# Weight casts queued beside other ScalarE work, and a weight load cut into quarters, in a streaming encoder layer

## The chip, the cores and the metric

The kernel runs on one core of a Trainium2 chip. The metric is the device time of one execution in microseconds (us); lower is better. The engines are named as in the profile: PE (TensorE, matrix multiplication; PEld is its weight load), ACT (ScalarE), DVE (VectorE), POOL (GpSimd) and SP (SyncE, which here only issues DMA transfers). Each engine works through its own queue in order.

## The reference

One layer of a streaming encoder, for 1024 prompt tokens and 8 decode streams of 16 tokens. The width is 1024; there are 8 heads of 64 with stick-breaking attention (group A) and 8 heads of 64 with banded chunk attention (group B).

```python
def trunk_layer(x, p, ...):
    h = rmsnorm(x, g_mix)
    q_a, k_a, v_a, q_b, k_b, v_b = split_heads(h, w_in)
    a = stick_breaking(q_a, k_a, v_a, ...)       # with the cached past for the decode streams
    o_b = band_attention(q_b, k_b, v_b, ...)
    a = rmsnorm(a, g_out_sb)
    o_b = rmsnorm(o_b, g_out_cb)
    x = x + concat(a, o_b) @ w_out
    h = rmsnorm(x, g_ffn)
    x = x + (silu(h @ w_gate) * (h @ w_up)) @ w_down
    gate = sigmoid(rmsnorm(x, g_ple) @ w_ple_gate)
    x = x + gate * (p @ w_ple_proj)
    return x, new

def stick_breaking(q, k, v, q_pos, k_pos):
    z = einsum('bqhd,bkhd->bhqk', q, k) * HEAD_DIM ** -0.5
    causal = k_pos[None, :] < q_pos[:, None]
    log_keep = where(causal, log_sigmoid(-z), 0.0)
    between = cumsum(log_keep, axis=3, reverse=True) - log_keep
    w = where(causal, exp(log_sigmoid(z) + between), 0.0)
    return einsum('bhqk,bkhd->bqhd', w, v)
```

## The kernel before

All data is float32. A product of two float32 matrices is made of three fast products: each operand is split into a high part, rounded by a cast (on ACT), and a low part, the difference (on POOL or DVE); `mm3` (L101 to L104) multiplies high by high, high by low and low by high. So every weight chunk costs a load into `wraw`, a cast to `whi` and a subtraction to `wlo`. A chunk is 128 x 2048 elements (1 MB); it is cast and subtracted in parts, mostly quarters of 128 x 512. There is one raw buffer, so the next load starts when the last subtraction has read the one before; there are two buffers of high and low parts.

The tokens are nine tiles of 128 rows: eight of the prompt, one that holds the decode streams. The stages, with their rough times in the profile:

- 0 to 130: norm of the rows, transposes, first chunks of the projection.
- 130 to 290: the other projection chunks (12 of 256 columns in all) beside the stick-breaking attention of the decode streams, `decode(0, ...)`. The order of PE is that of the code here; the other engines' orders come from a list scheduler with a model of times.
- 290 to 510: the last projection chunks beside the stick-breaking attention of the prompt, `attention` (`advance(project, att, 1.95)`). The scheduler orders all engines.
- 510 to 806: the banded attention of the decode streams and of the prompt and, beside the latter, the first half of the output product (`half_out`).
- 806 to 870: second half of the output product (`lower`), row by row, with the norm and the transposes for the next stage. PE's order is that of the code from the third row on.
- 870 to 1340: gate and up product; 1340 to 1590: down product; then the gate by the layer's input embedding and the final norm.

What the change touches:

- `Chunks.beside` (L162 to L176) runs a projection chunk's units (one unit is one product of a token tile, or of three for queries) and, from the second unit on, casts one quarter of the next chunk after each of four units (L174), with the subtraction on POOL. When the products of a unit are copied out of PSUM, ACT does it for every other tile (`st`, L296) and for the transposed keys and queries (`transposed_out`, L253 and L256).
- In the decode attention DVE weighs the scores (`wdec`, L463); POOL copies the last 16 columns to `wn` (L475), which PE transposes (L433).
- In the attention of the prompt POOL multiplies `w` by `keep` (L605, stick-breaking), or ACT takes the exponential (L607, banded), and PE transposes `w` (L623).
- `half_out` (L1002 to L1025) follows the string `ORDER`. "t" is a transpose of one head pair's mixed heads for three tiles (`turn_mix`: PE L867, then `hUh` on ACT L870 and `hUl` on DVE L871), "u0" and "u1" make a tile of the left or right 512 columns, a number such as "50" waits for head pair 5 and transposes its first group; "r" loads the second output weights (right columns), "p" casts and subtracts them in four parts.
- `lower` (L1092 to L1098) adds the second half of the output product to a tile `xa` or `xb` and stores it to `x1d`. Two rows later `weighed` multiplies `xa` by the norm's weights in place on POOL (L1109), so it must wait for that store. ACT takes the squares (`T4h`, L1104) and scales `hrow` (L1122), which PE transposes (L1130).
- `gate_up(0)` (L1220, load at L143) fetches the first gate chunk; `part_of` (L1081) casts it, one half at the eighth row and one at the end.

Of the kernel before, what the change touches and what calls it, by code (L numbers as in the profile page):

```python
# [13 lines left out]
F32 = mybir.dt.float32  # L14
# [8 lines left out]
P = 128  # L23
D = 1024
KT = 8
# [7 lines left out]
SKEW = 2  # L33
R2 = 1.2
LAG, RAWS, PT = 5, 7, 2
FIRST = 2
ORDER = ("u0 40 t u0 41 t u0 42 t t r u0 t u0 t t u0 t u0 p 50 u0 51 u0 52 "
         "u1 60 u1 61 u1 62 u1 u1 u1 u1 u1 u1")
VLAG, AHEAD = (2, 1), 2

# [2 lines left out]
def tile_hymba_step(  # L43
# [82 lines left out]
    def load_row(pool, src, tag):  # L126
        t_ = pool.tile([P, D], F32, name="row_" + tag, tag=tag)
        nc.sync.dma_start(t_, src.broadcast_to([P, D]))
        return t_

    class Chunks:


# [31 lines left out]
        def beside(self, units, src, k, n, first):  # L165

            v = self.raw(src, k, n)
            h, l = self.pair(k, n)
            for i, _ in enumerate(units):
                yield  # L170
                j = i - first
                if 0 <= j < 4:
                    o = slice(j * k // 4, (j + 1) * k // 4)
                    A.copy(h[:, o], v[:, o])  # L174
                    sub(G, l[:, o], v[:, o], h[:, o])
            return h, l  # L176

# [68 lines left out]
    def qkv(ch, hT, stg, first, second):  # L246

        def transposed_out(grp, w, c, g, src, scale=1.0):
            both = stg.tile([P, 2, 384], F32R, name="sq", tag="sq")
            n = min(384, NP * P - g * 384)  # L250
            hl = [both[:, x, :n] for x in range(2)]
            if scale == 1.0:
                A.copy(hl[0], src[:, :n])  # L253
                sub(V, hl[1], src[:, :n], hl[0])
            else:
                A.activation(hl[0], src[:, :n], AF.Copy, scale=scale)  # L256
                V.scalar_tensor_tensor(hl[1], src[:, :n], scale, hl[0].bitcast(F32), op0=ALU.mult, op1=ALU.subtract)
            for x in range(2):
                sent.append(nc.sync.dma_start(qkT[grp][w][x][c, :, g * 384 : g * 384 + n], hl[x].bitcast(F32)))
            if n < 384:  # L260
                new = both[:, 0, n:].bitcast(F32)
                A.activation(new, src[:, n:], AF.Copy, scale=scale)
                nc.sync.dma_start(fresh[grp][w][c], new)
# [23 lines left out]
        def others(grp, w, c, wts, gs):  # L287

            wh, wl = wts
            for g in gs:  # L290
                st = stg.tile([P, 3, 256], F32, name="st", tag="st", bufs=2)
                for o in range(3):
                    ps_ = ps["o"].tile([P, 256], F32, name="ps", tag="O")
                    for k in range(KT):
                        mm3(ps_, *hT.tok(g * 3 + o, k), wh[:, k], wl[:, k], k == 0, k == KT - 1)
                    (V.tensor_copy if o % 2 else A.copy)(st[:, o], ps_)  # L296
                    if w == 2 and g * 3 + o < NP:
                        values_out(grp, c, g * 3 + o, st[:, o])
                    yield
                if w == 1:  # L300
                    for pr in range(2):
                        pt = ps["t"].tile([P, 384], F32, name="pt", tag="T")
                        for o in range(3):
                            T.transpose(pt[:, o * P : (o + 1) * P], st[:, o, pr * P : (pr + 1) * P], ident)
                        transposed_out(grp, 1, c * 2 + pr, g, pt)
                first = 4 if grp else 0
                ts_ = [t for t in range(g * 3, g * 3 + 3) if first <= t < NP]
                if ts_:
                    lo, hi = ts_[0], ts_[-1] + 1
                    nc.sync.dma_start(  # L310
                        kv_prompt[grp, w][0, 0, (lo - first) * P : (hi - first) * P, c * 4 : c * 4 + 4, :]
                        .rearrange("(t p) h d -> p t (h d)", p=P),
                        st[:, lo - g * 3 : hi - g * 3],
                    )
                if g == 2:
                    nc.sync.dma_start(
                        kv_sample[grp, w][0, :, :, c * 4 : c * 4 + 4, :].rearrange("b i h d -> (b i) (h d)"),
                        st[:, 2],
                    )
                    if w == 2:  # L320
                        nc.sync.dma_start(fresh_v[grp][c], st[:, 2])
# [207 lines left out]
            yield  # L529


    kept, last = [], [None, None]

    def attention(ap_, ps, lag):
# [40 lines left out]
        def scores(st, hh, t):  # L575
# [28 lines left out]
                G.memset(w[:, n - 1 :], 0.0)  # L604
                kept.append(G.tensor_tensor(w[:, : n - 1], w[:, : n - 1], keep[:, 1:], op=ALU.mult))  # L605
            else:
                A.activation(w, w, AF.Exp, bias=mx, scale=-1.0, accum_out=st["rs"][:, hh, t : t + 1])  # L607
            return w

        def flip(st, hh, t, w):  # L610
# [390 lines left out]

    def half_out():  # L1002

        turns = [(k, g) for g in (1, 2) for k in range(4)]
        nc.sync.dma_start(own, mixs[1])
        late = [fetch_mix(k, 2) for k in range(3)]
        place = {0: 0, 1: 0}
        for what in ORDER.split():
# [5 lines left out]
                half_weights.append(out_raw(0, 1))  # L1014
                continue
            elif what == "p":
                half_weights[1] = ch.parts(half_weights[1], 4, 512, 4)
                continue
            elif what[0] == "u":
                c = int(what[1])  # L1020
# [66 lines left out]
    def fetch(t, half):  # L1087
        x = xg.tile([P, 512], F32, name="x" + "ab"[half], tag="x" + "ab"[half], bufs=(4, 2)[half])
        nc.sync.dma_start(x, resid[t * P : (t + 1) * P, half * 512 : half * 512 + 512])
        xs[t, half] = x  # L1090

    def lower(t, half):  # L1092
        acc = bank()
        for k in range(4):
            mm3(acc, *hT.tok(t, 4 + k), w_b[half][0][:, k], w_b[half][1][:, k], k == 0, k == 3)
        x = xs[t, half]
        V.tensor_tensor(x, x, acc, op=ALU.add)
        nc.sync.dma_start(x1d[t * P : (t + 1) * P, half * 512 : half * 512 + 512], x)  # L1098

    def squares_of(t, i, x):  # L1100
        if not i:
# [107 lines left out]
    with ExitStack() as planned:  # L1209
        for i in range(NT + SKEW):  # L1210
# [6 lines left out]
                fetch(order[j + 1], 1)  # L1217
            if i < NT:
                lower(order[i], 0)
            if i == SKEW:  # L1220
                raw = gate_up(0)
            if j < 0:
                continue
            if j == 1:
# [614 lines left out]
```

## Time and profile before

| what | value |
|---|---|
| median of 3 runs | 1699.58 us (1699.13 to 1699.96) |
| the profiled run | 1700.87 us |
| span of the profiled run | 1698.6 us |
| granted PE clock, mean over the span | 0.990 |
| instructions | 27811 |
| DMA, bytes moved | 292.44 MB |

The profile is of one execution. A row of a timeline gives start, duration, engine, line, operation, what is written and read, the shape and, in brackets, how long the engine stood idle before it and what ended the wait. A window's row gives its length, each engine's busy time with its count of instructions, the granted clock of PE as a share of full speed, the DMA engines' busy share and the rate. The idle time of an engine matters only where PE, which is nearly always busy, waits for it.

### The profile page before, as it was taken

How to read it: one execution, taken by the hardware profiler on the slowest of the kernel's cores; microseconds unless marked ns; L12 is line 12 of the kernel's file. 1: busy time of each engine (PE TensorE's matmuls, PEld its weight loads, DVE VectorE, ACT ScalarE, POOL GpSimd, SP SyncE). 2: the span in 40 equal slices, each digit the busy share in tenths (PEclk: the TensorE clock that was granted, in tenths of full speed). 3: DMA queues.
4: the chain of work that ended last, by engine and by line, in shares of the span. 5: the costliest groups of instructions: out<-in, count | busy, mean ns of one | idle time of the engine just before them, and what ended most of it. 6: DMA issues, size and time to landing. Idle time of an engine off the chain costs nothing.

```text
span 1698.6 us, 27811 instructions
## 1 busy us (share of the span) xinstructions
PE 1650.3 (97%) x10308; PEld 1420.7 (84%) x10308; DVE 1067.9 (63%) x1674; ACT 815.5 (48%) x1758; POOL 830.6 (49%) x691
## 2 busy tenths in 40 slices
PE   8999999989998999999999999999999999999998
PEld 7999788889997777888778888888888788788887
DVE  5111444258788766674676666566665597898875
ACT  5324445267767776573763333323333344433673
POOL 2433311178555321032675555555555379868763
PEclk9999999999998999999999999999999999999999
DMA  5877798665458896863522222222222697713222
GB/s 194 276 243 219 251 292 284 185 199 159 131 153 258 236 278 183 233 180 131 199 75 96 97 96 96 96 96 96 96 97 82 226 365 246 263 68 122 90 99 100
DMA packets 173145, 292.44 MB, mean 172 GB/s; under 512 B 16849, under 2 KB 95825, under 8 KB 170706
## 3 DMA queue, kind: packets, MB, share of 16 engines
q1 hardware_dynamic: 173010, 290.67, 52.8%
q8 instruction: 82, 1.34, 0.3%
q14 instruction: 53, 0.43, 0.1%
HBM read 204.24 MB, written 86.38 MB: 171 GB/s over the span
## 4 chain that ended last, share of the span: by engine, by line
PE 83%; DMA 5%; DVE 4%; ACT 3%; POOL 2%; issue 2%; SPq 0%; POOLq 0%; ACTq 0%; DVEq 0%
PE ps L1171 26%; PE ps L102 7%; PE ps L103 7%; PE ps L104 7%; PE pt L1444 4%; PE pt L1171 4%; PE ps L1444 3%; PE pt L623 3%; PE pt L424 2%; PE acc L487 2%; PE po L647 2%; PE po L646 2%; PE sdec L446 2%; PE S L592 1%; PE S L593 1%
## 5 line engine op out<-in xcount | busy, mean ns | idle before, releaser
L107 POOL TENSOR_TENSOR wlo<-wraw,whi 128x512 fp32r<-128x512 f32 (+1 forms) x143 | 225.5, 1602 | 66.2 <-ACT whi L161 34.7
L102 PE MATMUL ps<-whi,hTh 128*128 128x256 f32 x576 | 168.5, 293 | 0.0
L104 PE MATMUL ps<-whi,hTl 128*128 128x256 f32 x576 | 164.8, 286 | 0.0
L103 PE MATMUL ps<-wlo,hTh 128*128 128x256 f32 x576 | 164.6, 286 | 0.0
L102 PEld LDWEIGHTS ps<-whi,hTh 128*128 128x128 f32 x576 | 111.2, 193 | 6.4 <-issue 6.1
L113 DVE TENSOR_TENSOR_SCAN keep<-keep,places 128x128 f32<-128x128 f32 (+4 forms) x64 | 95.2, 1492 | 33.4 <-ACT keep L596 32.9
L605 POOL TENSOR_TENSOR w<-w,keep 128x127 f32<-128x127 f32 (+4 forms) x64 | 86.9, 1365 | 55.1 <-DVE keep L113 33.8
L103 PEld LDWEIGHTS ps<-wlo,hTh 128*128 128x128 f32 x576 | 111.4, 193 | 0.3 <-issue 0.2
L104 PEld LDWEIGHTS ps<-whi,hTl 128*128 128x128 f32 x576 | 111.1, 193 | 0.4 <-DVE hTl L107 0.2
L107 DVE TENSOR_TENSOR wtl<-pt,wth 128x512 fp32r<-128x512 f32 (+1 forms) x192 | 94.4, 512 | 22.4 <-ACT wth L627 22.2
L623 PE MATMUL pt<-ident,w 128*128 128x128 f32 x528 | 90.7, 284 | 10.9 <-DVE wtl L107 4.0
L627 ACT CAST wth<-pt 128x512 fp32r<-128x512 f32 (+1 forms) x192 | 85.3, 469 | 30.6 <-PE pt L623 30.2
L161 ACT CAST whi<-wraw 128x512 fp32r<-128x512 f32 (+1 forms) x104 | 67.7, 671 | 65.1 <-PE ps L1171 27.7
L623 PEld LDWEIGHTS pt<-ident,w 128*128 128x128 f32 x528 | 64.8, 145 | 23.1 <-POOL w L605 4.3
L123 POOL TENSOR_TENSOR r_o<-r_o,nhalf 128x8 f32<-128x8 f32 x16 | 31.0, 1939 | 103.9 <-DVE r_o L122 103.7
L646 PE MATMUL po<-wth,vk 128*128 128x256 f32 (+1 forms) x304 | 77.1, 284 | 1.6 <-DVE wtl L107 1.5
L592 PE MATMUL S<-qk 128*128 128x384 f32 (+2 forms) x192 | 73.2, 384 | 4.9 <-ACT keep L596 2.7
L107 POOL TENSOR_TENSOR actl<-actr,acth 128x1024 fp32r<-128x1024 f32 (+1 forms) x22 | 59.4, 2702 | 34.7 <-DMA sr<-acts 20.7
L647 PE MATMUL po<-wtl,vk 128*128 128x256 f32 (+1 forms) x304 | 73.3, 285 | 0.0
L425 DVE COPY kT<-pt 128x512 f32<-128x512 f32 x48 | 33.0, 688 | 57.3 <-PE pt L424 53.3
L103 PE MATMUL ps<-hTl,whi 128*128 128x384 f32 x192 | 65.9, 343 | 0.0
L104 PE MATMUL ps<-hTh,wlo 128*128 128x384 f32 x192 | 65.4, 341 | 0.0
(458 smaller groups left out, 5337.0 us busy)
## 6 DMA issues: line engine op xcount, KB each, us to landing
draw<-in_cache_sb_k SPq DMA_DIRECT2D x32, 512.0 KB, 4.9
draw<-in_cache_sb_v SPq DMA_DIRECT2D x32, 512.0 KB, 7.8
act<-sg SPq DMA_DIRECT2D x11, 1152.0 KB
actr<-act SPq DMA_DIRECT2D x22, 576.0 KB, 9.1
wraw<-in_w_in SPq DMA_DIRECT2D x11, 1024.0 KB, 7.7
wraw<-in_w_gate SPq DMA_DIRECT2D x11, 1024.0 KB, 5.3
wraw<-in_w_up SPq DMA_DIRECT2D x11, 1024.0 KB
v<-sv SPq DMA_DIRECT2D x32, 256.0 KB, 3.8
```

Source lines behind the costliest of these rows:

```text
L102: T.matmul(out, lhsT=ah, rhs=bh, start=start, stop=False)
L103: T.matmul(out, lhsT=ah, rhs=bl, start=False, stop=False)
L104: T.matmul(out, lhsT=al, rhs=bh, start=False, stop=stop)
L107: return eng.tensor_tensor(out, a, hi.bitcast(F32), op=ALU.subtract)
L113: V.tensor_tensor_scan(rev, rev, own[:, ::-1], 0.0, op0=ALU.mult, op1=ALU.max)
L592: T.matmul(sc, lhsT=hd["qq"][:, qs], rhs=hd["kkh"][:, kc], start=True, stop=False)
L605: kept.append(G.tensor_tensor(w[:, : n - 1], w[:, : n - 1], keep[:, 1:], op=ALU.mult))
L623: T.transpose(pt[:, (c - c0) * P : (c - c0 + 1) * P], w[:, c * P : (c + 1) * P], ident)
L646: T.matmul(dst, lhsT=vs, rhs=wth[:, kb - base, c0:c1], start=(i == 0), stop=False)
L647: T.matmul(dst, lhsT=vs, rhs=wtl[:, kb - base, c0:c1], start=False, stop=(i == nkb - 1))
L1171: T.matmul(out, lhsT=a[x][:, k], rhs=b[y][:, k], start=(not more and k == 0 and n == 0), stop=(k == 3 and n == 2), skip_group_check=more)
L1444: T.matmul(out, lhsT=a[i][:, x, m * P : (m + 1) * P], rhs=b[j][:, x], start=(not more and x == 0 and n == 0), stop=(x == 1 and n == 2), sk ...
```

## The change

Three edits, all of which say where in a queue something is issued. `tc.issue_after(x)` makes the scheduler put what is issued inside it behind instruction x; here x is on the same engine each time, so no semaphore is added.

1. In `beside`, each quarter's cast goes behind the latest copy of a projection product on ACT.
2. "p" of `ORDER` is cut in four; each cast of a quarter of the second output weights goes behind the latest exponential, among the "u0" and the turns of head pair 5.
3. The first gate chunk's load is cut into four of 256 KB, for the rows four to seven of the stage; each goes out behind its row's store to `x1d`.

```diff
-ORDER = ("u0 40 t u0 41 t u0 42 t t r u0 t u0 t t u0 t u0 p 50 u0 51 u0 52 "
+ORDER = ("u0 40 t u0 41 t u0 42 t t r u0 t u0 t t u0 t u0 p 50 p u0 p 51 u0 p 52 "
          "u1 60 u1 61 u1 62 u1 u1 u1 u1 u1 u1")
...
+    after = [None]
...
                     o = slice(j * k // 4, (j + 1) * k // 4)
-                    A.copy(h[:, o], v[:, o])
+                    with tc.issue_after(after[0].ins):
+                        A.copy(h[:, o], v[:, o])
                     sub(G, l[:, o], v[:, o], h[:, o])
...
-                A.copy(hl[0], src[:, :n])
+                after[0] = A.copy(hl[0], src[:, :n])
...
-                A.activation(hl[0], src[:, :n], AF.Copy, scale=scale)
+                after[0] = A.activation(hl[0], src[:, :n], AF.Copy, scale=scale)
...
-                    (V.tensor_copy if o % 2 else A.copy)(st[:, o], ps_)
+                    copied = (V.tensor_copy if o % 2 else A.copy)(st[:, o], ps_)
+                    if o % 2 == 0:
+                        after[0] = copied
...
-                A.activation(w, w, AF.Exp, bias=mx, scale=-1.0, accum_out=st["rs"][:, hh, t : t + 1])
+                exps[0] = A.activation(w, w, AF.Exp, bias=mx, scale=-1.0, accum_out=st["rs"][:, hh, t : t + 1])
...
-        turns = [(k, g) for g in (1, 2) for k in range(4)]
+        turns, half_split = [(k, g) for g in (1, 2) for k in range(4)], [3, 2, 1, 0]
...
             elif what == "p":
-                half_weights[1] = ch.parts(half_weights[1], 4, 512, 4)
+                if len(half_weights) == 2:
+                    half_weights.append(ch.pair(4, 512))
+                k = half_split.pop()
+                h, l = [x[:, k] for x in half_weights[2]]
+                v = half_weights[1][:, k]
+                with tc.issue_after(exps[0].ins):
+                    A.copy(h, v)
+                sub(G, l, v, h)
+                if not half_split:
+                    half_weights[1] = half_weights.pop()
                 continue
...
-        nc.sync.dma_start(x1d[t * P : (t + 1) * P, half * 512 : half * 512 + 512], x)
+        stored[:] = [nc.sync.dma_start(x1d[t * P : (t + 1) * P, half * 512 : half * 512 + 512], x)]
...
-            if i == SKEW:
-                raw = gate_up(0)
+            if i == SKEW + 1:
+                raw = ch.pool.tile([P, 2048], F32, name="wraw", tag="wraw", bufs=1).rearrange("p (k n) -> p k n", k=KT)
+            if 0 <= i - SKEW - 1 < 4:
+                o = slice((i - SKEW - 1) * 2, (i - SKEW) * 2)
+                with tc.issue_after(stored[0].ins):
+                    nc.sync.dma_start(raw[:, o], cols(w_gate[0], 0)[:, o])
```

What this does to the queues, at three places. First POOL in the decode attention, at the first projection chunk that is cast beside it (168 us in the profile before); `wlo` are the subtractions of that chunk, `sv` those of the values, and `wn` is what PE waits for. Before:

```order
L107 TENSOR_TENSOR sv<-st,sv 128x4x64 x7
L107 TENSOR_TENSOR wlo<-wraw,whi 128x512 x4
L475 COPY wn<-wdec 128x16
L107 TENSOR_TENSOR sv<-st,sv 128x4x64
L473 MEMSET wn 128x128
```

And of the change, where `wn` is on L480:

```order
L107 TENSOR_TENSOR sv<-st,sv 128x4x64 x8
L480 COPY wn<-wdec 128x16
L478 MEMSET wn 128x128
L107 TENSOR_TENSOR wlo<-wraw,whi 128x512
L107 TENSOR_TENSOR sv<-st,sv 128x4x64 x2
L480 COPY wn<-wdec 128x16
L107 TENSOR_TENSOR wlo<-wraw,whi 128x512
L107 TENSOR_TENSOR sv<-st,sv 128x4x64
L107 TENSOR_TENSOR wlo<-wraw,whi 128x512
L478 MEMSET wn 128x128
L107 TENSOR_TENSOR wlo<-wraw,whi 128x512
```

The first `wn` has passed all four subtractions, and these come apart from each other.

Second ACT in the banded attention of the prompt, where the second output weights are cast (721 us). Before:

```order
L650 COPY ob<-po 128x256
L627 CAST wth<-pt 128x3x128
L607 ACTIVATE w,rsum<-w,mxp 128x640
L161 CAST whi<-wraw 128x512 x4
L870 ACTIVATE hUh_9258<-acc,g_out 128x384
L627 CAST wth<-pt 128x4x128
L669 ACTIVATE ob<-osb 128x512
```

Of the change, from the first of these casts on (now L1029; the exponential is L613, `hUh` L876):

```order
L613 ACTIVATE w,rsum<-w,mxp 128x256
L1029 CAST whi<-wraw 128x512
L633 CAST wth<-pt 128x128
L876 ACTIVATE hUh_9251<-acc,g_out 128x384
L633 CAST wth<-pt 128x4x128
L633 CAST wth<-pt 128x128
L613 ACTIVATE w,rsum<-w,mxp 128x384
L1029 CAST whi<-wraw 128x512
L613 ACTIVATE w,rsum<-w,mxp 128x512
L1029 CAST whi<-wraw 128x512
L656 COPY ob<-po 128x256
```

The four casts have come apart, the fourth stands nine rows further on behind an exponential of 640, and they begin some 20 rows after the `hUh` that they stood ahead of before.

Third ACT at the start of the norm of the rows (808 to 818 us), where `hrow` is what PE waits for. Before:

```order
L1104 ACTIVATE T4h,ss<-xa 128x4x128 x2
L1122 ACTIVATE hrow<-hrow,r_n 128x512
L1104 ACTIVATE T4h,ss<-xb 128x4x128
L1122 ACTIVATE hrow<-xa,r_n 128x512
L1225 ACT_TABLE_LOAD
```

Of the change (squares on L1121, `hrow` on L1139):

```order
L1121 ACTIVATE T4h,ss<-xa 128x4x128 x2
L1139 ACTIVATE hrow<-hrow,r_n 128x512
L1139 ACTIVATE hrow<-xa,r_n 128x512
L1246 ACT_TABLE_LOAD
L1246 ACTIVATE any<-nhalf 128x1
L1121 ACTIVATE T4h,ss<-xb 128x4x128
```

The squares of `xb` have moved behind `hrow` and the table load.

SP at the same place. Before:

```order
L143 DMA wraw<-in_w_gate 128x8x256
L1098 DMA x1d<-xa 128x512 x3
L1098 DMA x1d<-xb 128x512
L1098 DMA x1d<-xa 128x512
L1098 DMA x1d<-xb 128x512
```

Of the change (loads of x on L1104, stores on L1115):

```order
L1115 DMA x1d<-xa 128x512 x3
L1115 DMA x1d<-xb 128x512
L1115 DMA x1d<-xa 128x512
L1242 DMA wraw<-in_w_gate 128x2x256
L1104 DMA xb<-resid 128x512
L1104 DMA xa<-resid 128x512
L1115 DMA x1d<-xb 128x512
```

The gate chunk's first quarter comes behind five stores; the sixth store now stands behind two loads of rows. Besides these places the scheduler deals out PE, ACT, DVE and POOL anew from about 290 us to 510 us, where it is free to.

More of the change, by code (lines that the diff above doesn't have):

```diff
@@ L529, in decode @@
             yield
+    exps = [None]
     kept, last = [], [None, None]
@@ L1090, in fetch @@
         xs[t, half] = x
+    stored = []
     def lower(t, half):
```

## The prediction

> **What bounds the kernel now.** I read the page first, then the table of windows by stage, then the gaps of PE, then the same table in stretches of 3.41 us around each gap. On the page PE is busy for 1650.3 us of 1698.6 us; no other engine reaches two thirds of that. So time can only go where PE waits, or where its clock is down.
>
> ```profile
> PE 1650.3 (97%) x10308; PEld 1420.7 (84%) x10308; DVE 1067.9 (63%) x1674; ACT 815.5 (48%) x1758; POOL 830.6 (49%) x691
> ```
>
> The windows (us, PE busy, PEld, DVE, ACT, POOL, granted clock, DMA share, GB/s) say where. From 900 to 1300 PE has no gap at all, and a change ahead of that only shifts it. The lost time lies in a few places of 100 to 900.
>
> ```profile
> 100.00:200.00 100.00, 96.06 (x779) 89.43 (x781) 21.49 (x31) 35.65 (x90) 37.77 (x42) 0.97 0.72 227
> 300.00:400.00 100.00, 93.49 (x841) 87.52 (x839) 50.74 (x70) 52.14 (x141) 50.06 (x59) 0.98 0.65 183
> 500.00:600.00 100.00, 91.36 (x725) 76.05 (x724) 79.93 (x164) 75.67 (x197) 47.95 (x59) 0.91 0.84 243
> 700.00:800.00 100.00, 96.87 (x599) 85.67 (x598) 65.74 (x184) 55.98 (x139) 22.71 (x19) 0.98 0.55 167
> 900.00:1300.00 400.00, 400.00 (x1774) 330.87 (x1773) 245.22 (x293) 126.96 (x221) 209.50 (x148) 1.00 0.27 93
> ```
>
> A gap costs more than itself. Cut into 3.41 us on the grid on which the clock changes here, the same view (PE alone) shows that a stretch with little PE work is followed by stretches at clock 0.50.
>
> ```profile
> 171.43:174.84 3.41, 1.14 (x12) 1.00 0.92 266
> 174.84:178.25 3.41, 1.98 (x12) 0.50 0.74 171
> 178.25:181.67 3.42, 3.42 (x16) 0.50 0.94 295
> 359.17:362.58 3.41, 1.50 (x11) 1.00 0.42 146
> 362.58:365.99 3.41, 3.41 (x15) 0.50 0.23 41
> 550.31:553.72 3.41, 1.83 (x13) 1.00 0.92 273
> 553.72:557.13 3.41, 2.70 (x20) 0.50 1.03 228
> 724.39:727.80 3.41, 1.68 (x9) 1.00 0.75 211
> 727.80:731.22 3.42, 3.42 (x18) 0.50 1.05 242
> 813.13:816.54 3.41, 2.10 (x10) 1.00 0.51 194
> ```
>
> Stretches with 1.14, 1.50, 1.68 and 1.83 us of PE work were followed by the half clock, the one with 2.10 was not. At half clock PE does half the work, so each stretch loses half of its busy time: 1.71 us when full.
>
> **The change part by part.** It adds no arithmetic; it adds three more DMA issues and moves casts, subtractions and loads in their queues.
>
> *Projection weights, first place (168 to 182).* ACT casts four quarters at a stroke, POOL then subtracts four times, and POOL's copy into wn stands behind them.
>
> ```profile
> 168.12 1.86 ACT L174 CAST whi<-wraw 128x512 fp32r<-128x512 f32 x3
> 168.81 7.26 POOL L107 TENSOR_TENSOR wlo<-wraw,whi 128x512 fp32r<-128x512 f32 x4 [1.14 <-ACT whi L174]
> 170.36 2.15 DVE L463 TENSOR_TENSOR wdec<-wdec,keep 128x1039 f32<-128x1039 f32 x1
> 173.16 1.09 PE L424 MATMUL pt<-ident,draw 128*128 128x128 f32 x8 [1.68 <-DVE kT L425]
> 176.27 0.48 PE L433 MATMUL pt<-ident,wn 128*128 128x128 f32 x1 [2.02 <-POOL wn L475]
> ```
>
> The subtractions end at 168.81 + 7.26 = 176.07; PE gets wn at 176.27. But wdec, all that wn copies from, was there at 170.36 + 2.15 = 172.51. In the new order wn stands ahead of all four subtractions, so it is ready before PE has done its transposes at 174.25, and the 2.02 us go. The gap of 1.68 us ahead of them is DVE's and stays. So the stretch 171.43 to 174.84 would hold 3.41 − 1.68 = 1.73 us of PE work, between the 1.68 and 1.83 that cost the clock: it still falls, for one full stretch (1.71) and not for two (1.98 / 2 + 1.71 = 2.70). Gain 2.02 + 0.99 = **3.0 us**; 4.7 if the clock holds, 2.0 if two stretches stay slow. [...]
>
> *Projection weights, later places.* From 200 to 300 the casts come in the same bunches and PE has no gap, so nothing is to be had. At 360 there is one:
>
> ```profile
> 358.18 1.30 POOL L107 TENSOR_TENSOR wlo<-wraw,whi 128x512 fp32r<-128x512 f32 x1
> 359.43 3.00 POOL L605 TENSOR_TENSOR w<-w,keep 128x767 f32<-128x767 f32 x1
> 362.48 0.86 PE L623 MATMUL pt<-ident,w 128*128 128x128 f32 x3 [1.91 <-POOL w L605]
> ```
>
> Here 1.91 us and a half-clock stretch (1.71) are 3.6. In the new order these casts lie behind copies that before came at 360.7 and later. That frees POOL for the w of 767, but puts the subtractions beside the next, wider rows of the attention. PE's order is free in this stage and is dealt out anew over some 300 us. Bounds: +3.6 if the stall goes, −3.6 if one like it comes on top. The work on POOL is the same and only changes its neighbour, so I take **0**.
>
> The last set is where the change adds a wait. Before, its casts started at 406.76; now each stands behind a query copy, the last behind the one at 453.62. These weights are needed once the sixth copy's matmuls (to about 460.8) are done.
>
> ```profile
> 406.76 0.69 ACT L174 CAST whi<-wraw 128x512 fp32r<-128x512 f32 x1
> 453.62 0.52 ACT L256 ACTIVATE sq<-ps 128x384 fp32r<-128x384 f32 x1
> 461.21 0.38 ACT L256 ACTIVATE sq<-ps 128x256 fp32r<-128x256 f32 x1
> ```
>
> From 454.1: a cast (0.69), a subtraction (1.30 to, in the worst row above, 7.26 / 4 = 1.8) and, if POOL has just begun a w, up to 3.00 of waiting: ready between 456.1 and 459.6. It is covered by the sixth group of query matmuls, with 1.2 us to spare in the worst case. I take 0, and a loss of 1 us as the end.
>
> *Second output weights (711 to 732).* The four casts wait on ACT for a load, and everything behind them on ACT waits too.
>
> ```profile
> 721.04 2.18 ACT L161 CAST whi<-wraw 128x512 fp32r<-128x512 f32 x4 [3.21 <-DMA wraw<-in_w_out]
> 723.74 0.62 DVE L871 SCALAR_TENSOR_TENSOR hUl<-acc,g_out,hUh 128x384 fp32r<-128x384 f32 x1 [3.59 <-ACT hUh L870]
> 724.41 0.55 PE L867 MATMUL acc<-ident,mixn 128*128 128x128 f32 x3 [0.91 <-DVE hUl L871]
> 726.32 0.33 PE L623 MATMUL pt<-ident,w 128*128 128x128 f32 x1 [0.60 <-ACT ob L650]
> 727.62 0.45 PE L646 MATMUL po<-wth,vk 128*128 128x256 f32 x1 [0.97 <-DVE wtl L107]
> ```
>
> ACT stands idle for 3.21 us and casts for 2.18 while hUh, wth and ob queue; PE pays 0.91 + 0.60 + 0.97 = 2.48 and then a half-clock stretch, 1.71. In the new order hUh and the copies pass, and each cast (0.55) comes alone, behind a later exponential, when the load has long landed. Gain **4.2 us**; at least 2.5 if only the gaps go and another late cast costs the clock. The price is that these weights are ready later, and the two loads behind them in the single raw buffer too; the first rows that need them stand behind all four casts in the order, and no row shows PE waiting on such weights now, so I take 0.
>
> *First gate chunk (806 to 818).* One load of 1 MB goes out just ahead of the stores of x1d. POOL multiplies xa in place, so it must wait for the store of xa.
>
> ```profile
> 806.36 0.38 SPq L143 DMA_DIRECT2D wraw<-in_w_gate  x1
> 808.24 2.10 SPq L1098 DMA_DIRECT2D x1d<-xa  x3
> 815.19 3.74 POOL L1109 TENSOR_TENSOR xa<-xa,row_grow 128x512 f32<-128x512 f32 x3 [2.66 <-DMA x1d<-xa]
> 816.05 0.63 ACT L1104 ACTIVATE T4h<-xb 128x512 fp32r<-128x512 f32 x1 [2.67 <-DVE xb L1097]
> 817.44 1.09 PE L1130 MATMUL pt<-ident,hrow 128*128 128x128 f32 x8 [2.21 <-ACT hrow L1122]
> ```
>
> POOL waited 2.66 us for the store; ACT then took the squares of xb ahead of hrow. In the new order both are gone from the front: no gate load stands ahead of the first five stores, and hrow comes before those squares. Both must move to give the whole **2.2 us**; with hrow alone behind POOL's first product (815.19 + 3.74 / 3 = 816.44, where ACT began at 816.68) only 0.2 is had, which is the lower end. The clock did not fall here. The quarters go out behind later stores.
>
> ```profile
> DMA to landing us min/median/max: 2.0/4.1/6.2
> 834.89 0.38 SPq L1098 DMA_DIRECT2D x1d<-xa  x1
> 845.15 1.15 ACT L1081 CAST whi<-wraw 128x512 fp32r<-128x512 f32 x2
> ```
>
> The stores of x1d, also 256 KB, land within 6.2 us, so the last quarter (behind the store at 834.89) is there by 841.5, ahead of the first cast at 845.15: cost 0. [...]
>
> **Sum:** 3.0 + 0 + 4.2 + 2.2 = 9.4 us. The profiled run took 1700.87 us (span 1698.6 and 2.3 around it), 1.3 above the median of 1699.58; 1700.87 − 9.4 = 1691.5 for such a run, and **1690.2 us** for the median.
>
> **The rivals.** (1) *The stalls come back in the free stretch.* The subtractions land beside wider rows at 360 to 460, and two stalls like the one at 360 (3.6 each) appear: 1690.2 + 7.2 = 1697.4, no change that can be measured. For it: POOL was wholly busy from 359.17 to 362.58, as the rows of 358.18 and 359.43 show. Against: 400 to 500 is dense PE work. (2) *Slower: the turn from the first attention to the next stage grows.* It is the worst stretch of the kernel, and nothing in the change aims at it, but the new order reaches it.
>
> ```profile
> 510.00:560.00 50.00, 41.36 (x297) 33.75 (x296) 43.36 (x66) 40.84 (x100) 27.53 (x38) 0.83 0.87 255
> ```
>
> PE idles 8.64 us, and a clock of 0.83 over 41.36 busy us loses about 7.0: 15.6. If projections lag behind their casts, or run out earlier, more of the widest attention rows meet a DVE that is 87% busy without matmuls to cover them. A second such stretch gives 1690.2 + 15.6 = 1705.8; slower by a measurable amount begins where it costs 12.8 more than now. Against: the added order is within ACT's own queue, behind copies that come anyway. (3) *Faster still:* that same turn loses half of its cost, 7.8, in the new order: 1682.4. Nothing aims at it, but it can fall as it can rise. That the edits don't do what they say is excluded by the order for wn, for the output casts and for hrow.
>
> **How the numbers follow.** Forecast 0.55 (1684 to 1696), rival 1 0.17, rival 2 0.12, rival 3 0.15, the rest beyond. A measurement of this kernel tells about 0.2%, 3.4 us, from no change: 1696.2 to 1703.0. Faster is the forecast, rival 3 and the lower edge of rival 1: 0.71; same 0.17; slower 0.12. The forecast's own bounds are 1690.2 − 1.7 − 3.6 = 1684.9, and, with 1.0 more at the first place, 1.7 at the second output weights, 2.0 at the gate chunk and 1.0 for the late last set, 1695.9. The range reaches towards rivals 3 and 1: 1681 to 1701.
>
> **What would show it.** In the profile after: no wait of PE on wn at the first place, the clock down for one stretch there; ACT with no wait on in_w_out ahead of hUh, no half clock near 728; hrow about 2 us earlier with POOL's wait for x1d short. Wrong would be: PE waiting on wlo at the head of the last projection chunk (late casts), on w or wtl for more than the 15.1 us of gaps that 300 to 400 and 510 to 560 show now (100 − 93.49 and 50 − 41.36), or on the gate weights after 845.

## The result and the profile after

The changed kernel takes 1688.09 us (median of 6 runs, 1686.38 to 1690.41), the kernel before 1699.77 in the same comparison (6 runs). The ratio is 0.9934, with a 95% interval of 0.9921 to 0.9947: 11.7 us less. The forecast was 1690.2 us. Measured once more beside a later experiment, the same two kernels gave 0.9916 (0.9900 to 0.9933).

The page of the changed kernel shows the same picture as before: PE is busy for nearly the whole span, but the span is 11.6 us shorter. PE's busy time fell by 8.6 us although no matmul was removed: that is mostly work which ran at half clock before (by the table below the half clock cost 12.7 us before and 4.9 after).

```profile
span 1687.0 us, 27813 instructions
PE 1641.7 (97%) x10308; PEld 1415.0 (84%) x10308; DVE 1063.2 (63%) x1674; ACT 813.4 (48%) x1758; POOL 825.9 (49%) x691
```

The windows of the stages say where it went. First the kernel before, then the changed one (PE alone: us, PE busy, granted clock, DMA share, GB/s). All borders lie where PE works without a gap in both kernels, so they can be the same although the second runs up to 13 us ahead.

```profile
130.00:164.00 34.00, 33.76 (x288) 1.00 0.75 231
164.00:182.00 18.00, 14.30 (x107) 0.81 0.74 223
321.00:407.00 86.00, 79.49 (x639) 0.98 0.65 182
509.00:564.00 55.00, 46.36 (x346) 0.84 0.87 257
564.00:676.00 112.00, 110.97 (x1001) 1.00 0.78 237
709.00:737.00 28.00, 25.38 (x159) 0.94 0.94 259
796.00:830.00 34.00, 31.45 (x151) 1.00 0.62 209
```

```profile
130.00:164.00 34.00, 32.30 (x273) 1.00 0.75 237
164.00:182.00 18.00, 17.86 (x176) 1.00 0.66 207
321.00:407.00 86.00, 79.58 (x617) 0.98 0.68 190
509.00:564.00 55.00, 46.78 (x372) 0.97 0.94 272
564.00:676.00 112.00, 109.40 (x983) 0.98 0.75 226
709.00:737.00 28.00, 28.00 (x194) 1.00 0.77 229
796.00:830.00 34.00, 32.85 (x161) 1.00 0.66 222
```

As a sum, with a loss counted as a window's length less PE's busy time, and half of the busy time inside the stretches at clock 0.5 (idle + clock, in us; the stretches are read from the trace). The half is an estimate: in the kernel before, successive matmuls of 128x256 mostly start 0.21 us apart inside these stretches and 0.12 us apart outside them.

| stage | before | after | change | forecast |
|---|---|---|---|---|
| 130 to 164, prologue's end | 0.2 + 0 | 1.7 + 0 | +1.5 | 0 |
| 164 to 182, first place | 3.7 + 2.7 | 0.1 + 0 | −6.3 | −3.0 |
| 321 to 407, prompt's attention | 6.5 + 1.7 | 6.4 + 1.7 | −0.1 | 0 |
| 509 to 564, the turn | 8.6 + 6.6 | 8.2 + 1.5 | −5.5 | 0 |
| 564 to 676 | 1.0 + 0 | 2.6 + 1.7 | +3.3 | 0 |
| 709 to 737, second output weights | 2.6 + 1.7 | 0 + 0 | −4.3 | −4.2 |
| 796 to 830, ahead of hrow | 2.55 + 0 | 1.15 + 0 | −1.4 | −2.2 |

These seven make −12.8; small changes elsewhere bring the loss from the start to 1600 us to −11.0, from 53.0 to 42.0. Such sums are not exact: the span less all its losses should be the same for each of the fourteen traces of this study, and it lies between 1636.3 and 1641.0 us, so that a difference of a few us between two spans need not show as gaps and clock. The rows that answer to those shown of before stand in three places. At the first, in the timeline of the changed kernel:

```profile
171.86 1.24 DVE L468 TENSOR_TENSOR wdec<-wdec,keep 128x1039 f32<-128x1039 f32 x1
172.50 1.19 POOL L107 TENSOR_TENSOR sv<-st,sv 128x256 fp32r<-128x256 f32 x1 [3.33 <-ACT sv L286]
172.97 1.45 PE L429 MATMUL pt<-ident,draw 128*128 128x128 f32 x8
173.64 0.19 POOL L480 COPY wn<-wdec 128x16 f32<-128x16 f32 x1
174.25 0.27 PE L438 MATMUL pt<-ident,wn 128*128 128x128 f32 x1
```

No wait stands at either PE row. What the reader is to see besides is the first row: DVE's product takes 1.24 us where it took 2.15, and here no weight subtraction runs on POOL. At the second place PE has no wait from 709 to 737 (28.00 busy of 28.00). The transposes behind which it waited for DVE go through, and the first of the four casts comes only at 745, with no wait for the load:

```profile
716.83 0.49 PE L873 MATMUL acc<-ident,mixn 128*128 128x128 f32 x3
745.00 0.61 ACT L1029 CAST whi<-wraw 128x512 fp32r<-128x512 f32 x1
```

At the third place, ahead of hrow:

```profile
796.82 0.69 DVE L1114 TENSOR_TENSOR xa<-xa,ps 128x512 f32<-128x512 f32 x1 [1.24 <-DMA xa<-resid]
797.53 2.35 SPq L1115 DMA_DIRECT2D x1d<-xa  x3
802.24 0.39 SPq L1242 DMA_DIRECT2D wraw<-in_w_gate  x1
802.71 3.76 POOL L1126 TENSOR_TENSOR xa<-xa,row_grow 128x512 f32<-128x512 f32 x3 [0.55 <-DMA x1d<-xb]
804.80 1.09 PE L1147 MATMUL pt<-ident,hrow 128*128 128x128 f32 x8 [1.15 <-ACT hrow L1139]
```

POOL's wait for the store fell from 2.66 to 0.55 us, PE's wait for hrow from 2.21 to 1.15; the first row itself now comes late for DVE, by 1.24. And two waits are new, one at the end of the prologue and one at 625, where ACT now does for the first output weights what it did before for the second:

```profile
138.92 0.39 PE L102 MATMUL ps<-whi,hTh 128*128 128x256 f32 x1 [1.10 <-ACT st L299]
624.66 2.18 ACT L163 CAST whi<-wraw 128x512 fp32r<-128x512 f32 x4 [3.80 <-DMA wraw<-in_w_out]
627.76 0.33 PE L921 MATMUL pt<-ident,pn 128*128 128x128 f32 x1 [2.37 <-ACT ob L656]
```

### The profile page after: what moved, and what is told of

Read it like the earlier page. It is cut to its first block, busy times and chain, and to the rows that moved or that the text cites. A ratio compares the mean times of both kernels' runs of the same rounds, so it can differ in the third digit from the quotient of the medians.

```text
span 1687.0 us, 27813 instructions
## 1 busy us (share of the span) xinstructions
PE 1641.7 (97%) x10308; PEld 1415.0 (84%) x10308; DVE 1063.2 (63%) x1674; ACT 813.4 (48%) x1758; POOL 825.9 (49%) x691
## 4 chain that ended last, share of the span: by engine, by line
PE 79%; DMA 6%; DVE 5%; POOL 4%; ACT 3%; issue 3%; SPq 0%; POOLq 0%; DVEq 0%; ACTq 0%
PE ps L1188 26%; PE ps L102 6%; PE ps L104 6%; PE ps L103 6%; PE pt L1465 4%; PE pt L1188 4%; PE ps L1465 3%; PE pt L629 2%; PE pt L429 2%; PE po L653 2%; DMA gated<-q 2%; PE acc L492 1%; DVE keep L113 1%; PE po L652 1%; PE sdec L451 1%
## 5 line engine op out<-in xcount | busy, mean ns | idle before, releaser
L107 POOL TENSOR_TENSOR wlo<-wraw,whi 128x512 fp32r<-128x512 f32 (+1 forms) x143 | 217.6, 1543 | 104.9 <-ACT whi L177 47.8
L102 PE MATMUL ps<-hTh,whi 128*128 128x384 f32 x192 | 65.0, 338 | 0.0
```

Of the source, the lines that this page charges most:

```text
L102: T.matmul(out, lhsT=ah, rhs=bh, start=start, stop=False)
L107: return eng.tensor_tensor(out, a, hi.bitcast(F32), op=ALU.subtract)
```

## The experiments

Each ratio is to the kernel before, measured on the same chip in the same rounds.

### One part at a time

`e1_casts` has the edits of `beside` and the three copies only, `e2_out` those of "p" and `ORDER` only, `e3_gate` those of the gate chunk only (the diff of the change, cut at these seams).

> Part 1 alone. By the gaps and half-clock stretches of the two traces, this part has the first place (6.3 us), pays 1.5 us near 137, and moves everything from 290 on: about 5.5 won from 510 to 565 and 3.3 lost from 565 to 680. Theory: all of these come with part 1 alone, so 6 to 7 us less than the kernel before, the 2.2 us ahead of hrow and the stall near 724 unchanged. Rival: the free stretch from 290 on owes its new order to the later edits as well; then only the first place and the 1.5 us show, about 4.8 us less, and 510 to 565 is as before.

> Part 2 alone. Theory: ACT no longer stands before the load of the second output weights, the three gaps of PE near 724 (2.5 us) and the half-clock stretch behind them (1.7) go: 4.2 us less than before, nothing else moves. Rival: the later weights cost something in the second half of the output product, and less than 3 us are left.

> Part 3 alone. Theory: the wait for hrow falls from 2.2 us to about 1.1 as in the changed kernel, because POOL still waits for a store; 1.1 us less than before and no other stage changes. Rival: the rest of the wait in the changed kernel comes from part 2's late weights (the second loads end later), and alone this part wins the whole 2.2 us.

Measured: part 1 alone 0.9967 (0.9957 to 0.9978; 1695.07 us), part 2 alone 0.9991 (0.9982 to 1.0000; 1699.20), part 3 alone 0.9993 (0.9983 to 1.0002; 1699.11). Part 1 does bring both of the things that nothing aimed at: the turn loses 8.2 + 1.6 and the stage behind it 2.4 + 1.7. Its time, 5.1 us less, falls short of the 6 to 7 expected; in its profiled run the unchanged gaps near 724 and ahead of hrow cost 4.9 us of clock, where they cost 1.7 in the kernel before. The gains of parts 2 and 3 alone are at the edge of what was measured: their intervals end at 1.0000 and 1.0002. Part 2 takes every gap near 724 and the half clock behind them, 4.3 us, as expected, and yet wins only about 1.5 by the ratio. Its timeline shows why:

```profile
799.95 0.38 SPq L143 DMA_DIRECT2D wraw<-in_w_gate  x1
800.42 0.53 SPq L128 DMA_DIRECT2D row_grow<-in_g_ffn  x1
801.01 1.69 SPq L1099 DMA_DIRECT2D xa<-resid  x3
807.69 0.69 DVE L1107 TENSOR_TENSOR xa<-xa,ps 128x512 f32<-128x512 f32 x1 [5.52 <-DMA xa<-resid]
808.43 0.50 PE L102 MATMUL ps<-whi,hUh 128*128 128x512 f32 x1 [3.63 <-DVE xa L1107]
```

Before, the 1 MB of the gate chunk went out after the loads of the first rows (806.36 against 800.44). With part 2 the raw buffer comes free earlier in relation to these rows, the load slips ahead of them, and the first row arrives 5.5 us late for DVE. PE waits 3.63 us, and 1.7 more are lost to the clock, 5.34 in this stage where the kernel before lost 2.55: 2.8 of the 4.3 us won at 724 are given back at 808. Part 3 alone shows no wait for hrow at all (a loss of 0.3 us from 796 to 830), so the rival was right there: with part 2, something of that wait is left. The 2.2 us that go there don't all show in its time, which is 1.0 us shorter by the medians and 1.2 by the ratio; where the rest went is not shown.

### Parts 2 and 3 together, and the gate chunk in one piece

`e10_out_gate` is the change without part 1. `e6_gate_whole` is the kernel before with (besides the line that keeps the latest store)

```diff
-            if i == SKEW:
-                raw = gate_up(0)
+            if i == SKEW + 1:
+                with tc.issue_after(stored[0].ins):
+                    raw = gate_up(0)
```

> Parts 2 and 3 without part 1. In the run of part 2 alone, the gate chunk's 1 MB load went out at 799.95, ahead of the loads of the first rows, and PE waited 3.6 us for the first row at 805; the 4.2 us won near 724 were lost again. Theory: part 3 takes that load out of the way, so the wait for the first row is gone or near it, 4.2 us are won near 724 and 1 to 2 ahead of hrow: 5 to 6.5 us less than before. Rival: the wait for the first row comes from the second output weights themselves, which are ready later; then it stays and less than 2.5 us are won.

> The kernel before, with the gate chunk's load in one piece of 1 MB, behind the store of the fourth row. Theory: what held hrow up was the load ahead of the stores, not its size; the 2.2 us ahead of hrow go as in the run of part 3 alone, and as nothing waits for the rows behind it, the time is that run's within 1.5 us. Rival: 1 MB in one piece delays the loads and stores of the next rows, and PE waits 1 us or more for one of them between 818 and 850, which the quarters avoid.

Measured: parts 2 and 3 together 0.9967 (0.9955 to 0.9978; 1694.55 us), about 5.1 us less, where each alone gave 1 to 1.5, neither clear of zero. The wait for the first row is gone, that for hrow is 0.65 us. So the two parts need each other: part 3 clears the way that part 2 had led the load into. One piece of 1 MB, only moved, gives 0.9988 (0.9978 to 0.9999); it too loses 0.3 us from 796 to 830, and no new wait appears up to 850. What counted in part 3 is the place of the load, not the quarters.

### The second output weights late, but in a bunch

`e11_late_gate` has part 3, and in place of part 2:

```diff
-... u0 t u0 p 50 u0 51 u0 52
+... u0 t u0 50 u0 51 u0 52 p
...
-                half_weights[1] = ch.parts(half_weights[1], 4, 512, 4)
+                h, l = ch.pair(4, 512)
+                v = half_weights[1]
+                for k in range(4):
+                    with tc.issue_after(exps[0].ins):
+                        A.copy(h[:, k], v[:, k])
+                    sub(G, l[:, k], v[:, k], h[:, k])
+                half_weights[1] = h, l
```

> Part 3, and in place of part 2 the four casts of the second output weights in one bunch, behind the latest exponential, after the last left half-tile. Theory: what counted was that ACT stood before a load that had not landed, not that four casts come together; so no wait near 724, less than 1 us of new gaps where the bunch stands, and the time of parts 2 and 3 within 1.5 us. Rival: the bunch of 2.2 us on ACT holds up the copies behind it just as before and PE loses 2 us or more there.

Measured: 1.0003 (0.9991 to 1.0014; 1699.96 us). The gaps near 724 are gone. The bunch of 2.16 us itself, with its load long landed, has two gaps of 0.9 us beside it, at 762 and 767, and no fall of the clock: less than the 2.5 and the stretch at half clock at 724, so most of the loss there came of ACT's stand before the load. But everything is lost again further on, by another way than the rival named:

```profile
762.20 2.16 ACT L1022 CAST whi<-wraw 128x512 fp32r<-128x512 f32 x4
```

```profile
762.85 0.50 PE L102 MATMUL acc<-whi,hUh 128*128 128x512 f32 x1 [0.90 <-ACT whi L1022]
```

```profile
811.75 0.80 PE L102 MATMUL ps<-whi,hUh 128*128 128x512 f32 x1 [1.97 <-DVE xa L1106]
```

PE reaches the right half before its weights are there. POOL's last subtraction of them ends at 769.65, the next weight load through the raw buffer goes out at 769.68 (730.30 before), and further on the first rows are fetched at 805.88 (800.44 before) and PE waits for the first of them at 811; in all 6.7 us from 737 to 830, where the kernel before lost 2.55. The step from the late weights to the late rows was not tried by itself. The casts must come late enough for the load to have landed and early enough for the next load. Part 2's places lie between the two.

### The first place: POOL's queue, or POOL beside DVE

`e5_wn_dve` is the kernel before with

```diff
-            G.tensor_copy(wn[:, b * 16 : b * 16 + 16], st["w"][:, n_old:])
+            (V if grp == 0 else G).tensor_copy(wn[:, b * 16 : b * 16 + 16], st["w"][:, n_old:])
```

`e9_first_place` is the kernel before with part 1 switched on only from the start of the decode stage to its end.

> The kernel before, with the copy into wn moved from POOL to DVE in the decode streams of group A; the four casts and four subtractions stay in one bunch, PE's and ACT's orders there are the same. Theory: wn comes right after wdec, so PE's 2.0 us at wn go; DVE's product of 128x1039 still takes 2.1 us beside the subtractions on POOL (1.24 where none runs), so the 1.7 us ahead of the transposes stay, the 3.4 us around them hold about 1.7 us of PE work, and the clock falls for one stretch: 3.0 us less than before. Rival: the clock holds, as in the changed kernel, and 4.7 us go. Second rival: the product takes 1.24 us here too, so that its time has nothing to do with POOL.

> The kernel before with part 1 only where the projections run beside the decode streams. Theory: both gaps near 172 go (2.0 at wn, 1.7 at the transposes, since DVE's product no longer runs beside the subtractions and takes 1.24 us) and the half clock behind them: 5.3 to 6.4 us less than before by how the clock would have fallen, nothing else. Rival: the 1.7 us ahead of the transposes stay, as they did with wn on DVE; then at most 4.7.

Measured: 0.9980 (0.9969 to 0.9990; 1697.39 us) for wn on DVE, 0.9958 (0.9942 to 0.9973; 1693.26) for part 1 here alone. With wn on DVE, its timeline has:

```profile
168.58 7.30 POOL L107 TENSOR_TENSOR wlo<-wraw,whi 128x512 fp32r<-128x512 f32 x4 [1.14 <-ACT whi L174]
```

```profile
170.13 2.14 DVE L463 TENSOR_TENSOR wdec<-wdec,keep 128x1039 f32<-128x1039 f32 x1
172.20 0.68 DVE L425 COPY kT<-pt 128x512 f32<-128x512 f32 x1
172.93 0.77 PE L424 MATMUL pt<-ident,draw 128*128 128x128 f32 x5 [1.68 <-DVE kT L425]
```

The bunch is still there, the product still takes 2.14 us, and the gap of 1.68 us ahead of the transposes is still there; only the one at wn has gone. With the bunch pulled apart (e9), the product takes 1.24 us and both gaps are gone. The median time of e9 is 7.4 us below that of the kernel before, more than the 6.3 lost here; in its profiled run the gaps near 724 also happened to cost no clock (2.2 + 0, against 2.6 + 1.7). So the first place held two faults of one bunch: POOL's queue kept wn back, and POOL's subtractions slowed DVE. The groups of the product in the kernel before and in the changed one (duration in ns, least, median and most) say the same:

```profile
L463 DVE TENSOR_TENSOR wdec<-wdec,keep x8: 1229/1241/2145, 170.4 to 310.0; 128x1039 f32<-128x1039 f32 x8
```

```profile
L468 DVE TENSOR_TENSOR wdec<-wdec,keep x8: 1231/1241/1243, 171.9 to 306.2; 128x1039 f32<-128x1039 f32 x8
```

Two of the eight took 2.14 us before, the two that ran beside weight subtractions from start to end; none does after. The slowing goes both ways. In the kernel before a subtraction of 128x512 beside which DVE did nothing took 1.27 to 1.30 us; of the four of the bunch, these two ran beside DVE's scan and product:

```profile
168.81 2.59 POOL L107 TENSOR_TENSOR wlo<-wraw,whi 128x512 fp32r<-128x512 f32 x1 [1.14 <-ACT whi L174]
171.37 2.27 POOL L107 TENSOR_TENSOR wlo<-wraw,whi 128x512 fp32r<-128x512 f32 x1
```

The ends alternate, 1.07 to 1.13 us apart: DVE's scan of keep at 170.33, the first subtraction at 171.40, DVE's product at 172.51, the second subtraction at 173.64.

The 0.9 us are not the whole of the 1.68. The eight transposes are two groups of four, each into one of two buffers `pt`, and each group waits until its buffer has been copied out, one by ACT and one by DVE. In the kernel before, the first group waits for DVE's copy (172.43 + 0.68 = 173.11, PE at 173.16), though ACT's had ended at 171.76. In the changed kernel (and in e9) it waits for ACT's, and only the second group for DVE's:

```profile
172.33 0.58 ACT L430 COPY kT<-pt 128x512 f32<-128x512 f32 x1
173.02 0.68 DVE L430 COPY kT<-pt 128x512 f32<-128x512 f32 x1
173.76 0.66 PE L429 MATMUL pt<-ident,draw 128*128 128x128 f32 x4
```

ACT's copy ends at 172.91 and PE starts at 172.97; DVE's ends at 173.70 and PE goes on at 173.76. So about half of the gap went with DVE's product and the rest with this change of buffers, which no edit asks for.

The clock in e5 was the second question. I had read from four stretches that some 1.75 us of PE work in 3.41 are too few to hold it. They were enough:

```profile
171.27:174.68 3.41, 1.75 (x19) 1.00 0.96 258
174.68:178.10 3.42, 3.42 (x35) 1.00 0.63 179
```

### Where part 1 is needed

`e4_dec_only` is the changed kernel with part 1 in the decode stage only; `e12_no_prologue` has it there and beside the prompt's attention, not in the prologue. Both use a switch that `beside` asks (e4 turns it off again ahead of the attention, e12 leaves it on):

```diff
+    beside_on = [False]
...
+                    if beside_on[0]:
+                        with tc.issue_after(after[0].ins):
+                            A.copy(h[:, o], v[:, o])
+                    else:
+                        A.copy(h[:, o], v[:, o])
...
+    beside_on[0] = True
     with tc.manual_schedule(engines={mybir.EngineType.PE}):
         advance(project, dec, R2, 30)
```

> The changed kernel with part 1 only where the projections run beside the decode streams (the first place), not in the prologue and not beside the prompt's attention. Theory: the first place keeps its 6.3 us, the 1.5 us near 137 are not paid, 4.2 come near 724 and 1 to 2 ahead of hrow, and from 321 to 676 the losses are those of the kernel before (about 24 us of gaps and half clock, against 21 in the changed kernel): about the changed kernel's time, within 3 us. Rival: the gain from 509 to 564 in the changed kernel hangs on anything that shifts the stage, and comes here as well; then 4 us or more less than the changed kernel.

> The changed kernel with part 1 beside the decode streams and beside the prompt's attention, but not in the prologue. Theory: only the two gaps near 137 (1.5 us) come from the prologue's casts; the better turn from 509 to 564 and the stall near 625 both come from the casts beside the attention and are as in the changed kernel: 1.5 us less than that, about 1686.6. Rival: the stall near 625 or the better turn hangs on the state that the prologue leaves behind; then one of the two is missing, and the time is 3 us or more away from that.

Measured: 0.9926 (0.9908 to 0.9945; 1688.18 us) and 0.9908 (0.9890 to 0.9927; 1685.33). Without part 1 in the prologue and beside the attention the changed kernel is as fast as with both. What the part beside the attention is worth is the step from e4 to e12. In e4 the turn and the stage behind it lose 8.5 + 3.8 and 0.8 + 0, 13.1 in all; in e12 they lose 8.2 + 1.5 and 2.7 + 1.7, 14.1. The better turn and the stall at 625 come together and nearly cancel. By the times e12 is 2.9 us the faster, with intervals that overlap; so whether that part helps is not settled. Without the prologue's part the two gaps near 137 are gone (0.2 us lost from 130 to 164), as expected. e12 is the fastest kernel of the study. Its interval and the changed kernel's overlap, so that the 1.5 us are shown by the gaps and not by the times.

### The first output weights treated likewise

`e15_changed` is the changed kernel once more. `e14_first_out` is e12 with, in the generator that casts the first output weights,

```diff
-        half_weights.append(ch.parts(v, 4, 512, 4))
+        h, l = ch.pair(4, 512)
+        for k in range(4):
+            with tc.issue_after(exps[0].ins):
+                A.copy(h[:, k], v[:, k])
+            sub(G, l[:, k], v[:, k], h[:, k])
+            if k < 3:
+                yield
+        half_weights.append((h, l))
```

> The changed kernel again, beside the next one on the same chip. Theory: 0.993 of the kernel before, as first measured; the stall near 625 and the gaps near 137 are there again, while the half-clock stretches differ by where the grid of 3.41 us happens to fall. Rival: the stall near 625 was of that one execution.

> The kernel without the prologue's part (part 1 beside the decode streams and the attention, parts 2 and 3), and the casts of the first output weights treated like those of the second: each quarter behind the latest exponential, one a step. Theory: ACT's wait of 3.9 us for that load ahead of the exponentials near 621 goes, and with it PE's 2.5 us and the half-clock stretch behind it (1.7): 3 to 4 us less than the kernel without the prologue's part, about 5 less than the changed kernel, 0.988 to 0.990 of the kernel before. Rival: as with the second weights in a late bunch, the later weights free the raw buffer later and something behind them (the mixed heads' loads, the first half-tiles) waits instead; then the gain is under 1.5 us.

Measured: 0.9916 (0.9900 to 0.9933; 1688.18 us) for the changed kernel, 0.9923 (0.9908 to 0.9937; 1688.77) for e14. The stall at 625 is in the repeated run as well (2.3 + 1.7). In e14 it is down to a wait of 0.9 at 624, and the rival's wait has taken its place: the raw buffer is free later, the mixed heads and the first rows of x, which use the same buffer, are fetched at 667 to 670, and the first half-tile waits for them:

```profile
667.54 0.33 SPq L919 DMA_DIRECT2D wraw<-mixp  x1
...
669.86 0.43 SPq L920 DMA_DIRECT2D wraw<-in_x_prompt  x1
```

```profile
676.54 0.50 PE L102 MATMUL acc<-whi,hUh 128*128 128x512 f32 x1 [1.80 <-DVE wraw L1017]
```

With a half-clock stretch behind it that is 3.5 us, and the gain is none.

## Why the prediction was right, point by point

The sign, the time and the range were right. The sum of 9.4 us stands against 11.7 in the times and 11.0 in the losses of the trace; but it is nearer than its terms. The first place gave 3.3 more than forecast, the gate chunk 0.8 less, and three places that stood at 0 gave −5.5, +3.3 and +1.5: that these nearly cancel is luck.

**The first place** was forecast at 3.0 and gave 6.3. The step that failed is "the gap of 1.68 us ahead of them is DVE's and stays". It was DVE's, but 0.9 of it because POOL held DVE up (2.15 against 1.24 us for the same product, e5 and e9), and the rest because the first transposes waited for DVE's copy and not for ACT's. The row for the first stood in the profile: a median of 1241 ns for this product, and 2.15 us in the timeline. Why the two slow each other is not shown. What was measured is 0.9 us lost by DVE here and, in the changed kernel, a subtraction of 128x256 on POOL that took 1.19 us beside the product, where it takes 0.74 in the kernel before at 166.94. The second step that failed is "between the 1.68 and 1.83 that cost the clock: it still falls": e5 held the clock with 1.75.

**The end of the prologue** was not in the sum. I looked for late weights at the end of the projections, where they did no harm (0.5 us from 407 to 509, on another engine's wait); they came at the prologue's end, where PE waited 0.36 us for a subtraction and 1.10 for a copy of st behind casts that come later: 1.5 us, which e12 takes away.

**The later places**, at 0, were right from 321 to 407, as a sum: the wait of 1.91 at 360 went, and one of 1.90 at 346 came, again with a stretch at half clock. The turn and the stage behind it come near 0 only if taken together (−2.2). Rival 3 named the turn as a thing that "can fall as it can rise"; it fell by 5.5, nearly all in clock (5.1), and 3.3 came back at 625. That this belongs to part 1 beside the attention is shown by e1, e4 and e12. Nine profiled runs with the old order there lost 3.6 to 7.2 us to the clock in this stage, five with the new one 1.5 to 1.7. The traces show how. In the old order waits of 1.54, 1.55 and 1.57 us follow each other within 9 us (522.8, 527.2 and 531.2 in the kernel before), so that the stretches at half clock are not full (1.86 and 1.84 us of PE work in the first two) and the clock stays down for three, from 526.42 to 536.66. In the new one a single wait of 2.46 stands at 518.8, the stretch behind it is nearly full, and the clock is back at 525.75 (first before, then after):

```profile
526.42:529.83 3.41, 1.86 (x10) 0.50 1.14 317
522.33:525.74 3.41, 3.09 (x15) 0.50 1.15 318
```

Why the scheduler's order came out so is not known.

**The second output weights** were forecast at 4.2 and gave 4.3 in the changed kernel. The cover was mis-stated, though: "the price is that these weights are ready later [...] so I take 0" holds only with part 3 beside it. Alone, the price was 2.8 us at 808 (e2).

**The gate chunk** was forecast at 2.2 and gave 1.4 (1.1 of the wait for hrow, and 0.3 of the small gap at 804). The mechanism was right: the load stood ahead of the stores (e3 and e6, 0.3 us left). A part of the wait stays in the changed kernel (0.6 to 1.15 in its two runs) and in all kernels with part 2; in the changed kernel the first row comes 1.24 us after DVE is ready for it. That the quarters as such would cost nothing was right, and they also bring nothing (e6).

Rival 1 (stalls come back in the free stretch) did not happen at 360 to 460, but a stall of its kind came at 625. Rival 2 did not happen.

## What to carry to other kernels

A bunch of casts and subtractions costs in three ways, and they must be counted apart: the queue that it blocks while it waits for its load (ACT, 3.21 us at 721), the queue behind its subtractions (POOL, where wn kept PE waiting for 2.02 us at 176), and the engine that its subtractions slow down (DVE, 0.9 us at 170). A shared raw buffer ties every cast to the next load: casts that come later for a good reason move a load, and what that load then stands ahead of, or behind, decides whether the gain stays (e2, e11, e14). So try edits to such a chain in pairs as well as alone; here two parts that gave 1 to 1.5 us each, hardly more than nothing, gave 5 together.

## What the runs showed of the hardware

- DVE's product wdec of 128x1039 took 1.23 to 1.24 us where no weight subtraction ran on POOL and 2.14 to 2.15 beside such subtractions; the two subtractions that ran beside DVE's scan and product in the kernel before took 2.59 and 2.27, others 1.27 to 1.30 alone.
- The clock changed on a grid of 3.41 us: in the kernel before it was down from 174.84 to 181.67 and from 362.58 to 365.99, in the changed kernel from 348.25 to 351.67. The grid is not tied to the program: in the kernel before the clock fell at 174.84, in e3 at 176.13 for the same gaps, and the first place cost 2.7 us of clock in the one and 1.6 in the other. In e1 the unchanged wait of 2.2 us for hrow was followed by a half-clock stretch, in the kernel before it was not. So a wait of about 2 us had no fixed price in these runs: it cost itself, and nothing or a stretch at half clock (up to 1.7 us) by where it fell.
- In these runs busy time alone didn't settle whether a stretch held the clock: 1.83 us of PE work did not at 550 in the kernel before, 1.75 did in e5. But the open range was narrow. Cut on each run's own grid from 15 us to some 1660, the fourteen traces have 6657 stretches at full clock: the clock fell behind all 30 with less than 1.5 us of PE work, behind 18 of the 32 with 1.5 to 1.9, and behind none of the other 6595.
- In these traces it took more PE work in a stretch to get the clock back than to keep it. Of the 77 stretches at half clock, all 26 in which PE was busy for less than 3.0 us were followed by another; the 43 with more than 3.3 were followed by the full clock; in between it went both ways (3 of 8 stayed down). So a wait inside a stretch at half clock could bring a further one: in the kernel before, the 2.02 us at wn left 1.98 us in the stretch from 174.84, and the clock stayed down to 181.67.
